# Layer 0's per-layer embedding moved from the end of the layer into its mixer, by way of memory

## The chip, the cores and the metric

The kernel runs on one core of a Trainium2 chip. Its engines work side by side, each through its own queue of instructions in order: TensorE (PE: matmuls and, listed as PEld, weight loads), VectorE (DVE), ScalarE (ACT), GpSimd (POOL) and SyncE (SP), which here issues nearly all the transfers (DMA). The metric is the device time of one execution in microseconds (us), lower is better. Times of several runs are given as their median.

## What is computed

One inference step of a two-layer encoder for 512 prompt rows and 32 sample rows (T = 544 columns in the kernel, which keeps features on partitions). Layer 0 has a mixer of a gated convolution and a state-space scan, then a convolutional feed-forward part; each layer ends with a gated embedding. Cut to what matters:

```python
z = hn @ W['w_even_in'][j]                       # 1024 -> 2048
gb, gc, xa, u = jnp.split(z, [A_WIDTH, 2 * A_WIDTH, 3 * A_WIDTH], axis=-1)
yc, new_hist = causal_dwconv(gc * xa, hist, W['w_conv_a'][j])
ya = gb * yc
yb, nr, ni = s5_mixer(u, ...)                    # scan over the rows, then a gate
y = jnp.concatenate([ya, yb], axis=-1) @ W['w_even_out'][j]
h = h + rmsnorm(y, W['g_mix_post'][i])
...
y = (jax.nn.gelu(gt) * val) @ W['w_ffn_down'][i]
h = h + rmsnorm(y, W['g_ffn_post'][i])
h = h + jax.nn.sigmoid(h @ W['w_ple_gate'][i]) * (pe[i] @ W['w_ple'][i])
```

The product `pe[i] @ W['w_ple'][i]` (256 features in, 1024 out) needs nothing that the layer computes.

## The kernel before

Every fp32 product is made of three matmuls on rounded operands: `mm_job` adds high x high (L131), low x high (L132) and high x low (L133) for each 128 rows of the sum. Weights come in units of 128x8x128: `prefetch` issues the load of `raw` on SP (L106), rounds it to `wh` on ACT (L107) and forms the rest `wl` on DVE (L108). The units are taken in the order of the list `units()`; four are kept at a time in the mixer, eight in the feed-forward part.

Columns are worked in two halves: half 0 is columns 0 to 255, half 1 columns 256 to 543 (288 wide). `phase(n, K, ...)` runs n weight units over both halves; half 1 of a unit is `delta` units behind half 0. A job is one unit on one half: 24 matmuls for K = 8. After each job it calls `run(rate)`, which advances the generators in the list `tasks` by that many steps, and takes results out of PSUM `lag` jobs late. So side work (norms, the scan) is spread over the jobs by counting calls; a scheduler then fixes each engine's order from when it thinks that operands are ready. An engine waits at the head of its queue, whatever stands behind.

Layer 0's mixer (`mixer_even`): phase(4) makes u. `shuffle` rearranges it on chip by 16 transfers on SP (`UUh`, L924). Then the generator `scan` runs beside phase(12), here called the a phase, whose 24 jobs make the convolution branch at rate 2. For each of eight pairs `scan` has `front` (matmuls `v`, L858; products `rt` with the rotation table E, L867 and L877; a scan instruction, L875; `sp`, L878 and L879) and `back` (matmuls `yp`, L891 and L893). It also makes its matrices: `prep_g` (transposes `tb`, L826, copied to `Bm` on ACT), `prep_c` (products Tm on DVE, copies `Cm` on ACT, L794) and `prep_t` (matmuls `tp`, L837, which need `Cm`). The table E is made by `rotations` on DVE, with copies on ACT. When all is done, the result of the scan is gated by matmuls on `GG`.

The tail of a layer (`tail`) ends with down products in three parts, then the embedding, then the gate. After the last part, `residual(half)` normalizes the down result y, adds it to h, and splits h into `Xh`, `Xl` for the gate, for eight slices k in turn (L338, L339, L323, L325). The embedding uses the unit p itself as the moving operand for half 0 (`pA`) and a copy with the sample rows attached for half 1 (`pB`), 8 jobs of 6 matmuls for each half, written to `e` by ACT (L472). The gate phase takes them in `c_gate` (L484).

Of the kernel before, what the change touches and what calls it, by code (L numbers as in the profile page):

```python
# [8 lines left out]
F32 = mybir.dt.float32  # L9
F32R = mybir.dt.float32r  # L10
I32 = mybir.dt.int32
AF = mybir.ActivationFunctionType
# [4 lines left out]
SEQ = 512  # L17
# [34 lines left out]

def units():

    u = [("w_even_in", i, 8) for i in range(16)]
    u += [("w_glu", i, 8) for i in range(2)]
    u += [("w_even_out", i, 8) for i in range(8)]
    for layer in range(2):
        for p, (a, b) in enumerate(FF_PARTS):
            u += [("w_up%d" % layer, i, 8) for i in range(2 * a, 2 * b)]  # L60
            u += [("w_down%d_%d" % (layer, p), i, b - a) for i in range(8)]
        u += [("p", layer, 8)]
        u += [("w_ple%d" % layer, i, 8) for i in range(2)]
        u += [("w_gate%d" % layer, i, 8) for i in range(8)]
        if layer == 0:
            u += [("w_odd_in", i, 8) for i in range(21)]
            u += [("w_odd_out", i, 8) for i in range(8)]
    return u
# [3 lines left out]
def trunk_kernel(ctx: ExitStack, tc: tile.TileContext, A: dict):  # L72
# [4 lines left out]
    main = ctx.enter_context(tc.tile_pool(name="main", bufs=1))  # L77
    small = ctx.enter_context(tc.tile_pool(name="small", bufs=2))
    mm = ctx.enter_context(tc.tile_pool(name="mm", bufs=3, space=PSUM))


    ulist = units()
# [5 lines left out]
    def wscope(n, extra=None):  # L88

        wsc.update(extra=extra, base=wsc["end"], end=wsc["end"] + n, ring=4 if extra is None else 8)  # L90
# [29 lines left out]
    def take(n):  # L120
        i = ucur[0]
        ucur[0] += n
        return list(range(i, i + n))
# [205 lines left out]
    def residual(half, h, y, st, gpost, gnext, rB=None):  # L329
# [18 lines left out]
            rB[half] = yield from s2.fin(D)  # L348
        waiting.discard(("r", half))


    def out_proj(layer, h, y, rB):

# [14 lines left out]
    def tail(layer, h, next_g):  # L368
# [2 lines left out]

        fs = ExitStack()
        ff = fs.enter_context(tc.tile_pool(name="ff%d" % layer, bufs=2))
        wscope(8 + 2 * NG + 24 + 11, fs.enter_context(tc.tile_pool(name="wf%d" % layer, bufs=4)))
        psc["extra"] = fs.enter_context(tc.tile_pool(name="fp%d" % layer, bufs=4, space=PSUM))
        psc["of"] = (7, 2)
        psc["st"] = fs.enter_context(tc.tile_pool(name="fs%d" % layer, bufs=1, space=PSUM))
# [11 lines left out]
        out_proj(layer, h, new_y(), rB)  # L389
        y = new_y()  # L390


        ps_r = ff.tile([128, 2, T - SEQ], F32, tag="psr", name="psr", bufs=1)
        nc.sync.dma_start(ps_r, A["ps"][layer])


        cg = [{}, {}]
# [54 lines left out]
        nc.sync.dma_start(A["o_ffn"][:, layer], fout[:, layer])  # L452


        us = take(3)
        prefetch(us[2])
        pA = [w_[:, :].rearrange("p (k t) c -> p k (t c)", k=2) for w_ in loaded[us[0]]]
        pB = [[ff.tile([128, T - 256], F32R, tag="ct%d" % i, name="pB", bufs=2) for k in range(2)] for i in range(2)]
        for k in range(2):
            for i in range(2):  # L460
                act.activation(pB[i][k][:, 0:256], pA[i][:, k, 256:512], AF.Copy)
            act.activation(pB[0][k][:, 256:], ps_r[:, k], AF.Copy)
            vec.tensor_tensor(pB[1][k][:, 256:], ps_r[:, k], pB[0][k][:, 256:], op=OP.subtract)
        emb = []
        for half, (c0, w) in enumerate(HALVES):
            e = ff.tile([128, 8, w], F32, tag="g%dh" % half, name="e", bufs=1)
            emb.append(e)
            xs = pA if half == 0 else pB
            for j in range(8):
                ps = ps_tile()  # L470
                mm_job(ps, us[1 + j // 4], range(2), xs[0], xs[1], 0, w, k0=2 * (j % 4))
                act.activation(e[:, j], ps[:, :w], AF.Copy, scale=0.5)  # L472
                run(j % 2)
        prefetch(us[2] + wsc["ring"])

        st = [Stat(0), Stat(1)]

# [40 lines left out]
    def mixer_even(h):  # L518
# [410 lines left out]
        task(scan())  # L929


        XCs = {}
        co = s5.tile([128, 4, 4], F32, tag="co", name="co")
        gct = [None, None]
# [420 lines left out]
        ms.close()  # L1355


    wscope(18)
    h = new_h()
    for half, (c0, w) in enumerate(HALVES):  # L1360
        for k0 in range(0, 8, 2 if half == 0 else 4):
# [157 lines left out]
```

## Time and profile before

| | us |
|---|---|
| runs, median of 3 (lowest to highest) | 1390.14 (1389.69 to 1393.61) |
| profiled execution | 1392.53 |
| its span (first to last instruction) | 1390.8 |
| PE busy | 1367.2 (98%) |
| DVE busy | 935.7 (67%) |
| ACT busy | 657.4 (47%) |

Busy is the time in which an engine executes, not its efficiency. In a timeline row the first number is the start from the span's start, the second the duration; `out<-in` are the kernel's names for the tiles, and a bracket at the end is idle time before the instruction with what ended it. Instructions of one engine overlap a little, so the step from start to start is shorter than a duration.

### The profile page before, as it was taken

The page shows a single profiled execution, that of the slowest core. Times are in us where ns is not written, and L with a number is a line of the kernel's source. Part 1 is how long each engine was busy: PE and PEld are TensorE (multiplying, and loading weights), DVE is VectorE, ACT ScalarE, POOL GpSimd, SP SyncE. Part 2 cuts the span into 40 slices and gives each one's busy share as a digit, 9 for nine tenths or more (in the row PEclk, how much of TensorE's full clock was granted, in tenths as well). Part 3 has the DMA queues.
Part 4 walks back from the last instruction along what each step waited for, and adds up shares of the span by engine and source line. Part 5 has one row for each costly group of instructions (what it writes and reads, how often), then busy time and mean ns, then how long its engine had stood idle before and what let it go on. Part 6 is the DMA issues. An engine that isn't in the chain of part 4 may idle for free.

```text
span 1390.8 us, 27437 instructions
## 1 busy us (share of the span) xinstructions
PE 1367.2 (98%) x10859; PEld 1344.2 (97%) x10859; DVE 935.7 (67%) x1968; ACT 657.4 (47%) x1314; POOL 198.3 (14%) x621
## 2 busy tenths in 40 slices
PE   8899999999999999999999999999999999999998
PEld 8798999999999999999998998999999999999998
DVE  9998738983477546868655555479843676368682
ACT  6653545543344223445547755465433343234451
POOL 1000000431022201300131100012320123013000
PEclk9999999999999999999999999999999999999999
DMA  6322352232312231331332332331223123313321
GB/s 199 94 67 63 117 184 77 77 96 72 122 62 86 97 122 39 105 113 53 99 94 70 117 109 64 108 107 62 92 92 122 46 92 107 99 50 94 100 73 50
DMA packets 49376, 128.26 MB, mean 92 GB/s; under 512 B 8368, under 2 KB 19896, under 8 KB 48992
## 3 DMA queue, kind: packets, MB, share of 16 engines
q1 hardware_dynamic: 47456, 124.35, 28.0%
q0 software_dynamic: 1792, 2.17, 0.7%
q8 instruction: 85, 1.39, 0.4%
q14 instruction: 43, 0.35, 0.1%
HBM read 116.93 MB, written 4.76 MB: 88 GB/s over the span
## 4 chain that ended last, share of the span: by engine, by line
PE 87%; DVE 8%; ACT 2%; SPq 1%; DMA 1%; issue 1%; POOL 0%; ACTq 0%; DVEq 0%
PE ps L131 27%; PE ps L133 27%; PE ps L132 27%; DVE wl L108 1%; SPq L924 1%; PE av L1254 1%; PE rp L307 1%; DVE Xl L327 1%; PE pp L1243 1%; DVE rg L875 1%; DVE rt L877 1%; ACT wh L107 1%; PE sc L1230 1%; DVE y L338 0%; DMA h<-in_x 0%
## 5 line engine op out<-in xcount | busy, mean ns | idle before, releaser
L131 PE MATMUL ps<-Xh,wh 128*128 128x256 f32 (+1 forms) x2512 | 728.1, 290 | 1.8 <-ACT wh L107 1.1
L133 PE MATMUL ps<-Xh,wl 128*128 128x256 f32 (+1 forms) x2512 | 725.5, 289 | 2.0 <-DVE wl L108 2.0
L132 PE MATMUL ps<-Xl,wh 128*128 128x256 f32 (+1 forms) x2512 | 725.6, 289 | 0.8 <-DVE Xl L327 0.5
L131 PEld LDWEIGHTS ps<-Xh,wh 128*128 128x128 f32 x2512 | 473.9, 189 | 4.4 <-ACT wh L107 1.6
L132 PEld LDWEIGHTS ps<-Xl,wh 128*128 128x128 f32 x2512 | 474.7, 189 | 3.0 <-DVE Xl L327 1.2
L133 PEld LDWEIGHTS ps<-Xh,wl 128*128 128x128 f32 x2512 | 473.0, 188 | 2.5 <-DVE wl L108 2.4
L108 DVE TENSOR_TENSOR wl<-raw,wh 128x1024 fp32r<-128x1024 f32 (+2 forms) x214 | 256.9, 1201 | 151.3 <-ACT wh L107 149.5
L107 ACT ACTIVATE wh<-raw 128x1024 fp32r<-128x1024 f32 (+2 forms) x214 | 222.1, 1039 | 248.3 <-PE ps L132 232.9
L131 PE MATMUL ps<-gh,wh 128*128 128x288 f32 (+1 forms) x704 | 203.5, 289 | 0.0
L133 PE MATMUL ps<-gh,wl 128*128 128x288 f32 (+1 forms) x704 | 203.4, 289 | 0.0
L132 PE MATMUL ps<-gl,wh 128*128 128x288 f32 (+1 forms) x704 | 202.5, 288 | 0.0
L132 PEld LDWEIGHTS ps<-gl,wh 128*128 128x128 f32 x704 | 133.5, 190 | 0.0
L131 PEld LDWEIGHTS ps<-gh,wh 128*128 128x128 f32 x704 | 133.0, 189 | 0.0
L133 PEld LDWEIGHTS ps<-gh,wl 128*128 128x128 f32 x704 | 132.9, 189 | 0.0
L278 ACT ACTIVATE t<-U,prm 128x256 f32<-128x256 f32 (+1 forms) x176 | 90.4, 517 | 71.0 <-DVE U L413 67.5
L279 DVE SCALAR_TENSOR_TENSOR t<-U,prm,t 128x256 f32<-128x256 f32 (+1 forms) x176 | 87.2, 498 | 34.9 <-ACT t L278 34.7
L413 DVE TENSOR_TENSOR U<-ps,rB 128x256 f32<-128x256 f32 (+1 forms) x176 | 76.6, 437 | 23.9 <-PE ps L133 19.8
L280 DVE SCALAR_TENSOR_TENSOR t<-U,prm,t 128x256 f32<-128x256 f32 (+1 forms) x176 | 87.5, 501 | 4.5
L416 POOL COPY hca<-U 128x2 f32<-128x2 f32 x88 | 24.3, 277 | 366.2 <-DVE U L413 366.1
L423 ACT ACTIVATE t<-t 128x288 f32<-128x288 f32 (+1 forms) x88 | 37.7, 429 | 81.6 <-DVE t L280 81.5
L439 DVE TENSOR_TENSOR y<-y,ps 128x256 f32<-128x256 f32 (+1 forms) x64 | 27.9, 436 | 62.0 <-PE ps L133 62.0
L429 ACT ACTIVATE gh<-t 128x288 fp32r<-128x288 f32 (+1 forms) x88 | 37.4, 425 | 67.3 <-DVE t L427 67.3
(272 smaller groups left out, 1376.7 us busy)
## 6 DMA issues: line engine op xcount, KB each, us to landing
raw<-in_w_up SPq DMA_DIRECT2D x88, 512.0 KB, 3.4
raw<-in_w_down SPq DMA_DIRECT2D x32, 512.0 KB, 3.4
raw<-in_w_odd_in SPq DMA_DIRECT2D x21, 512.0 KB, 3.6
raw<-in_w_gate SPq DMA_DIRECT2D x16, 512.0 KB, 4.0
raw<-in_w_even_in SPq DMA_DIRECT2D x15, 512.0 KB, 3.7
raw<-in_w_down SPq DMA_DIRECT2D x16, 384.0 KB, 3.1
raw<-in_w_even_out SPq DMA_DIRECT2D x8, 512.0 KB, 4.0
raw<-in_w_odd_out SPq DMA_DIRECT2D x8, 512.0 KB, 3.5
```

The source lines that it names most:

```text
L107: act.activation(wh[:, k], raw[:, k], AF.Copy)
L108: vec.tensor_tensor(wl[:, k], raw[:, k], wh[:, k], op=OP.subtract)
L131: pe.matmul(ps[:, :n], wh[:, k0 + k, :], h_, start=(i == 0), stop=False)
L132: pe.matmul(ps[:, :n], wh[:, k0 + k, :], l_, start=False, stop=False)
L133: pe.matmul(ps[:, :n], wl[:, k0 + k, :], h_, start=False, stop=(i == last))
L278: act.activation(t, v[2], AF.Copy, scale=w(2))
L279: vec.scalar_tensor_tensor(t, v[1], w(1), t, op0=OP.mult, op1=OP.add)
L280: vec.scalar_tensor_tensor(t, v[0], w(0), t, op0=OP.mult, op1=OP.add)
L413: vec.tensor_tensor(block_view(U, half)[2], like(ps, half), like(rB[half], half), op=OP.mult)
L423: act.activation(t, t, AF.Gelu_apprx_tanh)
L429: act.activation(gh[:, f - f0], g, AF.Copy)
L439: vec.tensor_tensor(yk, yk, ps, op=OP.add)
```

## The change

Layer 0's embedding is computed in the mixer, between phase(4) and the a phase, by a new function `embed`; layer 1's stays where it is and uses the same function. In the mixer the first eight jobs cover columns 0 to 287 (all from p), the other eight 288 to 543 (from `pB`, a buffer of the pool that the scan uses too). After each of the 16 jobs ACT writes `e` (one of three buffers), SP stores it to `emb0` in memory, and `run(1)` advances the scan by a step. In the tail two loads bring `emb0` back as `emb`. The units p and w_ple0 move to behind the fourth w_even_in unit.

```diff
-    u = [("w_even_in", i, 8) for i in range(16)]
+    u = [("w_even_in", i, 8) for i in range(4)]
+    u += [("p", 0, 8)]
+    u += [("w_ple0", i, 8) for i in range(2)]
+    u += [("w_even_in", i, 8) for i in range(4, 16)]
...
+    emb0 = dram.tile([128, 8, T], F32, tag="emb0", name="emb0")
...
+    def embed(ps_, pB, n0, put):
+
+        us = take(3)
+        prefetch(us[2])
+        pA = [w_[:, :].rearrange("p (k t) c -> p k (t c)", k=2) for w_ in loaded[us[0]]]
+        m = SEQ - n0
+        for k in range(2):
+            for i in range(2):
+                act.activation(pB[i][k][:, 0:m], pA[i][:, k, n0:SEQ], AF.Copy)
+            act.activation(pB[0][k][:, m:T - n0], ps_[:, k], AF.Copy)
+            vec.tensor_tensor(pB[1][k][:, m:T - n0], ps_[:, k], pB[0][k][:, m:T - n0], op=OP.subtract)
+        for n, (c0, w) in enumerate(((0, n0), (n0, T - n0))):
+            xs = pB if n else pA
+            for j in range(8):
+                ps = ps_tile()
+                mm_job(ps, us[1 + j // 4], range(2), xs[0], xs[1], 0, w, k0=2 * (j % 4))
+                put(n, j, c0, w, ps[:, :w])
+        prefetch(us[2] + wsc["ring"])
...
+        emb = [ff.tile([128, 8, w], F32, tag="g%dh" % half, name="e", bufs=1) for half, (_, w) in enumerate(HALVES)]
+        if layer == 0:
+            for half, (c0, w) in enumerate(HALVES):
+                nc.sync.dma_start(emb[half], emb0[:, :, c0:c0 + w])
+        else:
...
+            embed(ps_r, pB, 256, put_e)
...
+        ps_r = s5.tile([128, 2, T - SEQ], F32, tag="psr", name="psr")
+        nc.sync.dma_start(ps_r, A["ps"][0])
+        pB = pt([128, 2, 2, 256], "pB").bitcast(F32R)
+
+        def put_e(n, j, c0, w, ps):
+            e = small.tile([128, T - 256], F32, tag="sq", name="e", bufs=3)[:, :w]
+            act.activation(e, ps, AF.Copy, scale=0.5)
+            nc.sync.dma_start(emb0[:, j, c0:c0 + w], e)
+            run(1)
+
+        embed(ps_r, [[pB[:, i, k] for k in range(2)] for i in range(2)], 288, put_e)
```

Three places of the engines' orders. First SP's queue at the sixteen `UUh` moves that bring u into the scan's layout, before:

```order
L966 DMA hcs<-in_cache_ffn 128x176
L106 DMA raw<-in_w_even_in 128x1024 x5
L924 DMA UUh<-UUh 32x4x137 x16
L106 DMA raw<-in_w_even_in 128x1024 x2
L845 DMA Tm<-Tm 32x4x96
```

and of the change:

```order
L998 DMA hcs<-in_cache_ffn 128x176
L112 DMA raw<-in_w_ple 128x1024 x2
L112 DMA raw<-in_w_even_in 128x1024 x2
L958 DMA emb_69<-e 128x288 x3
L112 DMA raw<-in_w_even_in 128x1024
L943 DMA UUh<-UUh 32x4x137 x16
L958 DMA emb_69<-e 128x288 x5
L958 DMA emb_69<-e 128x256 x6
L112 DMA raw<-in_w_even_in 128x1024 x2
L864 DMA Tm<-Tm 32x4x96
```

Three stores and the weight load that was the last of five stand ahead of the moves now, the other stores behind them.

Second, PE at the end of the scan: the last `yp` among the a phase's matmuls (ps<-X), before:

```order
L891 MATMUL yp<-sp,Cm 128x137
L893 MATMUL yp<-UUh,Tm 128x137
L891 MATMUL yp<-sp,Cm 128x137 x2
L893 MATMUL yp<-UUh,Tm 128x137
L132 MATMUL ps<-Xl,wh 128x288
```

and of the change:

```order
L137 MATMUL ps<-Xh,wh 128x256
L910 MATMUL yp<-sp,Cm 128x137 x2
L912 MATMUL yp<-UUh,Tm 128x137
L910 MATMUL yp<-sp,Cm 128x137 x2
L912 MATMUL yp<-UUh,Tm 128x137
L138 MATMUL ps<-Xl,wh 128x256
```

From the last of these rows to the first matmul on `GG` stand 152 matmuls of the a phase before (104 of 288 columns, 48 of 256), and 335 in the change (192 and 143).

Third, PE between the last down matmul (ps<-gh) and the gate of layer 0, where L314 and L320 belong to the residual of half 0 and the rp<-ones,sq of the change to the statistics of half 1; before:

```order
L133 MATMUL ps<-gh,wl 128x288
L314 MATMUL rp<-cst,rc 128x128 x2
L131 MATMUL ps<-wh 128x256
L132 MATMUL ps<-wl,wh 128x256
L133 MATMUL ps<-wh,wl 128x256
```

and of the change:

```order
L139 MATMUL ps<-gh,wl 128x288
L320 MATMUL rp<-cst,rc 128x128 x2
L313 MATMUL rp<-ones,sq 128x1 x3
L137 MATMUL ps<-Xh,wh 128x256 x6
L138 MATMUL ps<-Xl,wh 128x256
```

The 96 matmuls of the embedding, of which ps<-wh is the first, are gone from there; the gate's matmuls on `Xh` follow at once.

## Rows read from the trace of the kernel before

**Rows 1.** The page's first lines: span; busy time of each engine (share) xinstructions

```profile
span 1390.8 us, 27437 instructions
PE 1367.2 (98%) x10859; PEld 1344.2 (97%) x10859; DVE 935.7 (67%) x1968; ACT 657.4 (47%) x1314; POOL 198.3 (14%) x621
```

**Rows 2.** Windows: length, busy (xinstructions) of PE, PEld, DVE, ACT, POOL; clock, DMA, GB/s

```profile
38.50:136.50 98.00, 87.27 (x683) 83.70 (x681) 90.57 (x183) 51.13 (x107) 1.03 (x10) 0.97 0.26 73
136.50:156.00 19.50, 19.50 (x154) 19.50 (x153) 13.22 (x25) 9.85 (x22) 0.00 (x0) 1.00 0.35 104
624.10:636.40 12.30, 12.30 (x100) 12.30 (x99) 11.58 (x28) 10.99 (x28) 0.00 (x0) 1.00 0.29 88
```

**Rows 3.** PE's waits, 38.5 to 136.5 us: us in total, times, longest

```profile
PE tp L837 <- ACT Cm L794: 4.5, 1, 4.5
```

**Rows 4.** Timeline of DVE: start us, us, engine, line, operation, shapes

```profile
42.61 0.22 DVE L593 TENSOR_TENSOR UUh<-ps,rB 128x32 f32<-128x32 f32 x1
57.35 1.29 DVE L867 TENSOR_TENSOR rt<-v,E 128x1096 f32<-128x1096 f32 x1
...
134.68 0.44 DVE L879 TENSOR_TENSOR sp<-rt 128x274 f32<-128x274 f32 x1
```

**Rows 5.** Window of the scan on DVE: length, busy (xinstructions), clock, DMA, GB/s

```profile
57.35:134.87 77.52, 70.19 (x131) 0.96 0.21 62
```

**Rows 6.** Timeline of PE: first matmuls of both embedding parts and of the gate

```profile
624.25 0.36 PE L131 MATMUL ps<-wh 128*128 128x256 f32 x1
...
630.08 0.30 PE L131 MATMUL ps<-pB,wh 128*128 128x288 f32 x1
...
636.48 0.28 PE L131 MATMUL ps<-Xh,wh 128*128 128x256 f32 x1
```

**Rows 7.** Timeline of DVE at the end of layer 0's down phase

```profile
626.42 0.48 DVE L338 SCALAR_TENSOR_TENSOR y<-y,prm,rB 128x256 f32<-128x256 f32 x1
...
634.65 1.23 DVE L108 TENSOR_TENSOR wl<-raw,wh 128x1024 fp32r<-128x1024 f32 x1
635.79 0.76 DVE L325 TENSOR_TENSOR Xl<-h,Xh 128x256 fp32r<-128x256 f32 x2
```

**Rows 8.** Timeline of SP's queue, and the chain that ended last, near 42 us

```profile
42.47 0.33 SPq L106 DMA_DIRECT2D raw<-in_w_even_in  x1
42.91 11.27 SPq L924 DMA_DIRECT2D UUh<-UUh  x16
...
52.09 1.92 DMA UUh<-UUh
```

**Rows 9.** Instructions on tile e; and the page's DMA issues

```profile
L472 ACT ACTIVATE e<-ps x16: 367/390/447, 625.7 to 637.5; 128x256 f32<-128x256 f32 x8, 128x288 f32<-128x288 f32 x8
...
raw<-in_w_gate SPq DMA_DIRECT2D x16, 512.0 KB, 4.0
```

**Rows 10.** Timeline of PE at 47 us and of ACT at 55 us

```profile
47.02 1.09 PE L826 MATMUL tb<-cst,G 128*128 128x128 f32 x8 [1.29 <-ACT G L821]
...
54.90 0.71 ACT L755 ACTIVATE E<-E 128x252 f32<-128x252 f32 x2
```

**Rows 11.** Groups of DVE in the scan: busy us, mean ns | idle before

```profile
L941 DVE TENSOR_TENSOR gct<-ps,rB 128x288 f32<-128x288 f32 (+1 forms) x6 | 2.5, 423 | 0.0
```

**Rows 12.** Timeline of PE behind the last yp; instructions on tile GG

```profile
136.65 0.29 PE L133 MATMUL ps<-Xh,wl 128*128 128x288 f32 x1
...
L131 PE MATMUL ps<-GG,wh x32: 284/290/294, 156.1 to 167.9; 128*128 128x274 f32 x32
```

**Rows 13.** Windows with the granted clock; timeline of PE at tp

```profile
60.00:65.00 5.00, 1.70 (x14) 1.50 (x12) 5.00 (x8) 2.45 (x4) 0.00 (x0) 0.89 0.00 0
65.00:70.00 5.00, 3.81 (x17) 2.87 (x18) 5.00 (x11) 3.59 (x6) 0.11 (x1) 0.50 0.00 0
70.00:75.00 5.00, 5.00 (x39) 5.00 (x40) 5.00 (x12) 2.35 (x4) 0.00 (x0) 0.93 0.42 128
...
66.19 3.62 PE L837 MATMUL tp<-Cm,g 128*32 128x128 f32 x16 [4.48 <-ACT Cm L794]
```

More of the change, by code (lines that the diff above doesn't have):

```diff
@@ L61, in units @@
             u += [("w_down%d_%d" % (layer, p), i, b - a) for i in range(8)]
-        u += [("p", layer, 8)]
-        u += [("w_ple%d" % layer, i, 8) for i in range(2)]
+        if layer == 1:
+            u += [("p", 1, 8)]
+            u += [("w_ple1", i, 8) for i in range(2)]
         u += [("w_gate%d" % layer, i, 8) for i in range(8)]
@@ L79, in trunk_kernel @@
     mm = ctx.enter_context(tc.tile_pool(name="mm", bufs=3, space=PSUM))
+    dram = ctx.enter_context(tc.tile_pool(name="dram", bufs=1, space=bass.MemoryType.DRAM))
+    emb0 = dram.tile([128, 8, T], F32, tag="emb0", name="emb0")
     ulist = units()
@@ L373, in tail @@
         ff = fs.enter_context(tc.tile_pool(name="ff%d" % layer, bufs=2))
-        wscope(8 + 2 * NG + 24 + 11, fs.enter_context(tc.tile_pool(name="wf%d" % layer, bufs=4)))
+        wscope(8 + 2 * NG + 24 + (11 if layer else 8), fs.enter_context(tc.tile_pool(name="wf%d" % layer, bufs=4)))
         psc["extra"] = fs.enter_context(tc.tile_pool(name="fp%d" % layer, bufs=4, space=PSUM))
@@ L390, in tail @@
         y = new_y()
-        ps_r = ff.tile([128, 2, T - SEQ], F32, tag="psr", name="psr", bufs=1)
-        nc.sync.dma_start(ps_r, A["ps"][layer])
+        if layer:
+            ps_r = ff.tile([128, 2, T - SEQ], F32, tag="psr", name="psr", bufs=1)
+            nc.sync.dma_start(ps_r, A["ps"][layer])
         cg = [{}, {}]
@@ L452, in tail @@
         nc.sync.dma_start(A["o_ffn"][:, layer], fout[:, layer])
[L455 to L472, printed above, removed]
+        emb = [ff.tile([128, 8, w], F32, tag="g%dh" % half, name="e", bufs=1) for half, (_, w) in enumerate(HALVES)]
[3 more added lines that the diff above has]
+        else:
+            pB = [[ff.tile([128, T - 256], F32R, tag="ct%d" % i, name="pB", bufs=2) for k in range(2)]
+                  for i in range(2)]
+            def put_e(n, j, c0, w, ps):
+                act.activation(emb[n][:, j], ps, AF.Copy, scale=0.5)
                 run(j % 2)
-        prefetch(us[2] + wsc["ring"])
+            embed(ps_r, pB, 256, put_e)
         st = [Stat(0), Stat(1)]
@@ L929, in mixer_even, with put_e @@
         task(scan())
+        ps_r = s5.tile([128, 2, T - SEQ], F32, tag="psr", name="psr")
+        nc.sync.dma_start(ps_r, A["ps"][0])
+        pB = pt([128, 2, 2, 256], "pB").bitcast(F32R)
+        def put_e(n, j, c0, w, ps):
+            e = small.tile([128, T - 256], F32, tag="sq", name="e", bufs=3)[:, :w]
[3 more added lines that the diff above has]
+        embed(ps_r, [[pB[:, i, k] for k in range(2)] for i in range(2)], 288, put_e)
         XCs = {}
@@ L1355, in mixer_odd @@
         ms.close()
-    wscope(18)
+    wscope(21)
     h = new_h()
```

## The prediction

> **What bounds the kernel now.** I read the page first: TensorE (PE) is busy 1367.2 of 1390.8 us [rows 1], so whatever takes PE's time off its path is worth that time, and an engine beside it costs nothing until PE waits for it. Next I read the busy time by stage, to see whether PE is as full where the work goes as where it leaves. It isn't. From the end of the u projection to the end of the scan (38.5 to 136.5 us) PE is busy 87.27 of 98.0 us and VectorE (DVE) 90.57; in the rest of the a phase (136.5 to 156) PE is busy all of its 19.5 us, and so it is in the embedding at 624.1 to 636.4 [rows 2]. The largest wait of PE in the scan stage is 4.5 us, before `tp` [rows 3]. The reader is to see that two works run side by side here: a scan, whose chain is DVE's, and the a phase, which fills PE while the scan's few matmuls wait in the same queue. The last u result is written at 42.61, the first product of the scan (`rt`, L867) starts at 57.35, and the last `sp` (L879) ends at 135.1 [rows 4]. Between those two DVE is busy 70.19 of 77.52 us [rows 5]: it, not PE, says when the scan ends. I call that end T.
>
> **The matmuls that move.** 48 matmuls of 256 columns start at 624.25, 48 of 288 at 630.08, and the first of the gate at 636.48 [rows 6]: 5.83 and 6.40 us, so 0.121 and 0.133 us each, 12.2 us in all. The mixer gets 48 of each width again, so PE's total work stays. What counts is what lies under which wait, before and after.
>
> **Tail of layer 0: 12.2 us leave, about 9 come back.** Before, the embedding ran on PE while DVE did `residual(0)`: its first instruction starts at 626.42, its last pair at 635.79, which ends at 636.55, with one weight split (`wl`, 634.65 to 635.79 by starts) among them [rows 7]. The gate's first job needs that result, slice k for its k-th triple. By the order of the change nothing but the statistics of half 1 stands between the last down matmul and the gate, and no `wl` stands inside the residual. So it ends 1.1 us earlier, near 635.4, the last triple follows, and the job ends near 635.8. Before, it began at 636.48 and took 24 x 0.121 = 2.9 us, to 639.4. The tail gives 639.4 - 635.8 = 3.6 us; half 1's statistics may take a little of it, so I count **-3.1**. Bounds: nothing, and the whole -12.2, if the residual could start so much earlier; its start hangs on the statistics of the last down results, and nothing in the change moves those.
>
> **The scan's start: about +3.** In SP's order of the change three stores of `e` and one weight load now stand ahead of the sixteen `UUh` moves. The third store needs the third `e`, and on ScalarE (ACT) that stands behind the E copies of rotation step 3, another `e` and a G copy. Before, the moves began at 42.91, right behind the last u result, took 11.27 us on SP, and the last landed at 52.09 + 1.92 = 54.0 [rows 8]. Now the last u result comes some 0.5 us later (one more pair of rotation products is ahead of it), E copies, G and two `e` take about 1.9 us on ACT and DVE (an `e` 0.39 [rows 9]), a store and a load about 1 us of SP (11.27 / 16 = 0.7, and 0.33 for a load [rows 8]): moves from 46.4, landed near 57.5. From there PE needs the first `v` matmul and the second `tb` group (1.09), ACT the `Bm` and E copies (1.0 and 0.7) [rows 10], because in the new order `tb` stands behind that `v`, and E behind `Bm`. `rt` can start near 60.4 instead of 57.35: +3.0. Bounds: 0, if DVE has as much other work as before until then, and +6, if `e` waits for its three buffers too (the nearest transfers land in 2 to 4 us).
>
> **The scan itself: about -3.5.** By DVE's order, between the first `rt` and the last `sp` stand 18 instructions of the a phase instead of 30, and two more E products. 12 x 0.37 us from start to start (the group has a mean of 0.42 with overlap [rows 11]) is -4.4, the two E products +0.9. DVE's waits in the stretch, 77.52 - 70.19 = 7.3 us [rows 5], I leave as they are; bounds: they vanish (-7.3) or double (+7.3). T then moves by 3.0 - 3.5 = **-0.5 us**.
>
> **What is left to do at T: +23.2.** This is the term that decides. The scan takes a step at each call of `run`: two per a job (24 matmuls, 3.0 us of PE), but one per embedding job (6 matmuls, 0.76 us). So sixteen of its steps now come with 16 x 0.76 = 12.2 us of PE work beside them, where before they had 16 x 1.5 = 24. PE's order shows it: before, 152 matmuls of the a phase stand behind the last `yp` (104 of 288, 48 of 256); now 335 do (192 and 143). The 152 took from 136.65 to the first GG matmul at 156.1, 19.45 us [rows 12]; the steps of 0.133 and 0.121 give 19.6 for them and 42.8 for the 335: **+23.2**, of which 12.2 is the embedding's time and 11.0 is work that no longer lies beside the scan. PE's idle time in the scan stage should double, from 10.7 to some 21 us.
>
> **The clock: +1.** After the 4.48 us wait before `tp` the granted clock stands at 0.50 from 65 to 70 and is 0.89 and 0.93 in the fives beside it [rows 13]: (0.11 + 0.50 + 0.07) x 5 = 3.4 us of full-speed time lost, most of it while PE waits or does `tp` (3.62 us for 16 matmuls). The longer waits can add such stretches, one in the mixer and one in the tail; the waits themselves are long gone on DVE's path, so I take 1, with 0 and 2 x 3.4 as bounds. The Trainium skill (TensorE: Matmul & The Clock Gate, section "HAM oscillation — how this bites in real kernels") says that waits between bursts of matmuls put the array back to its half rate each time, so that a wait costs more than itself. The trace agrees at 65 to 70; priced fully at both places that rule would make the sum 5.8 us larger.
>
> **Costed at nothing.** The two loads of `emb0` (1.0 and 1.2 MB): at the pace of a gate weight, 512 KB in 4.0 us [rows 9], 8 and 9 us. The first can start once half 0 of the down phase is done, seven jobs (7 x 18 x 0.133 = 17 us) before that phase ends, the second at 624, and half 1 of the gate needs it near 652 (5.7 jobs of 2.9 us after 635.8). Without that cover each us late is a us. The three weight units of the embedding take the a phase's ring slots, but sooner than the a phase asks for its fourth unit.
>
> **Sum.** -3.1 - 0.5 + 23.2 + 1 = **+20.6 us**. The profiled execution took 1392.53 us, 1.7 over its span and 2.4 over the median of the runs, 1390.14; the sum is a difference, so on the median it gives **1410.7 us**, +1.5%.
>
> **Rivals.**
> 1. *The gaps are filled; not slower.* PE's 10.7 us of idle in the scan stage [rows 2] swallow the embedding: mixer +12.2 - 10.7 = +1.5, tail -3.1: 1388.5 us, no change to measure; if the residual were also free in the tail, 1379.4. For it speaks that PE waits only where the work goes. Against it: T would have to come some 20 us earlier, at 114.5, while DVE alone has 66.7 us of work from the first `rt` on: 57.35 + 66.7 = 124. It decides at that point, T before 114.5. Chance 0.08 (0.04 same, 0.04 faster). The Trainium skill (Perfetto Trace Analysis, section "Optimization Strategy") advises to interleave stretches in which different engines are the most contended, which is this rival; the trace says that the place was already interleaved, with the a phase.
> 2. *The scan gains, or the tail does.* With fewer a results DVE's 7.3 us of waits vanish, or the tail keeps most of its 12.2: 1403 or 1401 us. For it: some of those waits are for PE. Chance 0.22.
> 3. *A new wait in the mixer.* Three `e` buffers, the store behind sixteen moves on the same queue, and ACT stuck at an `e` with the scan's copies behind it: T +7 and the clock +6, 1424 us. Chance 0.12.
> The forecast has 0.58.
>
> **Range.** A measurement here can tell about 0.3%, 4 us. The forecast's own bounds of a few us a term give some 1404 to 1417; to leave out no more than 2 in 10 it must take in rival 2 and half of 3: 1400 to 1421. Faster 0.04, same 0.04, slower 0.92.
>
> **What would show it.** Right: in the new profile some 14 a jobs run on a full PE after the last `yp`; GG starts 20 to 25 us later than 156.1; the `UUh` moves end near 57 or later; PE idles some 8 to 10 us between the last down matmul and the end of the gate's first job. Wrong: T far ahead of 130, a tail that closes without a gap, or a wait before GG for weights held up by the second set of moves on SP.

## The result, and the profile after

| | before | after |
|---|---|---|
| runs, median of 6 each (lowest to highest), us | 1392.34 (1389.69 to 1393.96) | 1400.62 (1399.32 to 1402.67) |
| span of the profiled execution, us | 1390.8 | 1399.1 |
| start of the first GG matmul | 156.05 | 171.15 |
| last instruction of PE's down phase of layer 0 | 624.12 | 637.73 |
| first matmul on `nid`, in layer 1's mixer | 718.0 | 726.5 |

The change makes the kernel slower: ratio 1.0064, 95% interval [1.0054, 1.0074], 8 to 9 us. The sign was forecast, the size was not: +20.6 was predicted. The table says where the time went: +15.1 up to GG, -1.5 from there to the end of the down phase, -5.1 in the tail, and -0.2 behind it, +8.3 in all.

The page's first lines after:

```profile
span 1399.1 us, 27490 instructions
PE 1370.5 (98%) x10859; PEld 1346.7 (96%) x10859; DVE 936.1 (67%) x1968; ACT 656.4 (47%) x1314; POOL 197.4 (14%) x621
```

PE has the same 10859 matmuls as in [rows 1], and is idle 28.6 us instead of 23.6. Where, two windows show (length; busy time and instructions of PE, PEld, DVE, ACT, POOL; clock; DMA share; GB/s). Before:

```profile
36.00:64.00 28.00, 24.41 (x197) 23.91 (x195) 28.00 (x73) 19.78 (x39) 0.11 (x1) 1.00 0.42 116
64.00:136.00 72.00, 64.86 (x500) 61.79 (x501) 64.67 (x123) 33.86 (x73) 0.93 (x9) 0.95 0.21 60
```

After:

```profile
36.00:64.00 28.00, 18.25 (x123) 16.58 (x122) 27.89 (x74) 22.95 (x47) 0.10 (x1) 0.87 0.49 144
64.00:136.00 72.00, 69.56 (x549) 66.84 (x549) 60.99 (x112) 37.01 (x82) 0.86 (x9) 0.98 0.27 79
```

The idle time has moved forward. At the scan's start, where the embedding now stands, PE idles 9.8 us instead of 3.6; behind 64 it idles 2.4 instead of 7.1. DVE has next to no gap at the start in either. So PE's idle time from 36 us to GG is 12.2 us, against 10.7; with the 12.2 us of embedding and some 1.2 more lost at the half clock (the busy time of each 4 us times what its clock lacks: 3.5 against 2.3) that makes the +15.1 but for 0.2.

The scan in the timeline of DVE after:

```profile
42.73 0.21 DVE L612 TENSOR_TENSOR UUh<-ps,rB 128x32 f32<-128x32 f32 x1
...
54.44 1.30 DVE L886 TENSOR_TENSOR rt<-v,E 128x1096 f32<-128x1096 f32 x1
...
126.88 0.42 DVE L898 TENSOR_TENSOR sp<-rt 128x274 f32<-128x274 f32 x1
```

Against [rows 4] the last u result stands where it stood, the first `rt` starts 2.9 us earlier, and T, the end of the last `sp`, is 127.3 instead of 135.1. SP's queue shows why the first of these is not the delay that was forecast:

```profile
40.83 1.78 SPq L958 DMA_DIRECT2D emb<-e  x3
42.72 0.39 SPq L112 DMA_DIRECT2D raw<-in_w_even_in  x1
43.20 10.43 SPq L943 DMA_DIRECT2D UUh<-UUh  x16
```

The three stores are ahead of the moves, but they are done by the time that u is: the moves start 0.3 us later than in [rows 8]. Behind T, the timeline of PE and the instructions on GG:

```profile
128.54 0.37 PE L138 MATMUL ps<-Xl,wh 128*128 128x256 f32 x1
...
L137 PE MATMUL ps<-GG,wh x32: 284/290/294, 171.1 to 183.0; 128*128 128x274 f32 x32
```

From that row to GG it is 42.6 us against the 19.45 of [rows 12]: +23.1, as counted. The longest waits of PE between 36 us and GG (engine, line, waited for; us, times, longest):

```profile
PE ps L137 <- ACT e L957: 4.0, 1, 4.0
PE tb L845 <- ACT G L840: 3.3, 3, 1.2
PE v L877 <- DVE rt L886: 2.7, 1, 2.7
PE yp L910 <- ACT GG L1009: 0.9, 1, 0.9
```

The wait at `tp` [rows 3] is gone and a wait for an `e` stands in its place. The timeline of ACT ahead of that `e`:

```profile
56.23 1.58 ACT L774 ACTIVATE E<-E 128x756 f32<-128x756 f32 x2 [1.89 <-DVE E L770]
57.72 1.06 ACT L891 ACTIVATE sp<-seg,sb 128x274 f32<-128x274 f32 x2
59.29 1.27 ACT L813 ACTIVATE Cm<-Tm 64x512 f32<-64x512 f32 x2 [0.51 <-DVE Tm L810]
60.58 0.99 ACT L957 ACTIVATE e<-ps 128x288 f32<-128x288 f32 x3
```

ACT waits for DVE's products E and Tm, and the copies that would free PSUM for the next embedding jobs stand behind them in its order (e4 below shows that the stores have a part in that order). In the tail, the timeline of PE, and two windows of it:

```profile
637.73 0.38 PE L320 MATMUL rp<-cst,rc 128*128 128x128 f32 x2
640.93 1.44 PE L313 MATMUL rp<-ones,sq 128*128 128x1 f32 x6 [2.82 <-DVE sq L304]
642.23 0.99 PE L137 MATMUL ps<-Xh,wh 128*128 128x256 f32 x3
```

```profile
640.00:645.00 5.00, 4.07 (x19) 4.07 (x20) 5.00 (x15) 1.59 (x4) 0.00 (x0) 0.56 0.74 245
645.00:650.00 5.00, 5.00 (x35) 5.00 (x35) 4.26 (x13) 1.59 (x4) 1.07 (x1) 0.76 0.03 11
```

PE waits only 3.6 us there (0.8 of it for `rc`), then takes the slices of several gate jobs in turn as the residual makes them; the clock costs 0.44 x 4.07 + 0.24 x 5 = 3.0 us of its busy time. 12.2 - 3.6 - 3.0 = 5.6, near the gain of 5.1.

### The profile page after: what moved, and what is told of

Read it like the earlier page. It is cut to its first block, busy times and chain, and to the rows that moved or that the text cites. A ratio compares the mean times of both kernels' runs of the same rounds, so it can differ in the third digit from the quotient of the medians.

```text
span 1399.1 us, 27490 instructions
## 1 busy us (share of the span) xinstructions
PE 1370.5 (98%) x10859; PEld 1346.7 (96%) x10859; DVE 936.1 (67%) x1968; ACT 656.4 (47%) x1314; POOL 197.4 (14%) x621
## 4 chain that ended last, share of the span: by engine, by line
PE 88%; DVE 8%; ACT 2%; issue 1%; POOL 1%; DMA 0%; SPq 0%; ACTq 0%; DVEq 0%; POOLq 0%
PE ps L137 27%; PE ps L138 27%; PE ps L139 27%; DVE wl L114 2%; PE av L1286 1%; DVE Xl L333 1%; ACT wh L113 1%; PE rp L313 1%; PE pp L1275 1%; PE sc L1262 1%; PE yp L910 1%; PE tp L856 0%; DVE y L344 0%; DVE h L345 0%; PE sc L1347 0%
## 5 line engine op out<-in xcount | busy, mean ns | idle before, releaser
L137 PEld LDWEIGHTS ps<-gh,wh 128*128 128x128 f32 x704 | 132.9, 189 | 0.0
L139 PEld LDWEIGHTS ps<-gh,wl 128*128 128x128 f32 x704 | 132.9, 189 | 0.0
```

Of the source, the lines that this page charges most:

```text
L137: pe.matmul(ps[:, :n], wh[:, k0 + k, :], h_, start=(i == 0), stop=False)
L139: pe.matmul(ps[:, :n], wl[:, k0 + k, :], h_, start=False, stop=(i == last))
```

## The experiments

Times are medians of 4 to 11 runs (before: 6 to 15), with the ratio to before on the same chip; u, T and GG are the end of the last u result, of the last `sp`, and the start of the first GG matmul in the profiled execution.

| kernel | median us | ratio [95%] | u | T | GG |
|---|---|---|---|---|---|
| before | | | 42.8 | 135.1 | 156.1 |
| after | 1400.62 | 1.0064 [1.0054, 1.0074] | 42.9 | 127.3 | 171.1 |
| e1_tail_alone | 1384.03 | 0.9950 [0.9936, 0.9965] | 42.6 | 133.7 | 154.7 |
| e2_mixer_alone | 1408.84 | 1.0119 [1.0105, 1.0133] | 44.6 | 128.1 | 171.9 |
| e3_no_steps | 1400.65 | 1.0066 [1.0053, 1.0079] | 44.6 | 152.3 | 173.3 |
| e4_no_store | 1399.70 | 1.0056 [1.0044, 1.0068] | 45.2 | 127.3 | 170.2 |
| e5_wl_pool_after | 1420.95 | 1.0204 [1.0190, 1.0218] | 48.0 | 143.4 | 190.3 |
| e6_wl_pool_before | 1402.24 | 1.0067 [1.0055, 1.0080] | 48.6 | 143.8 | 167.3 |
| e7_split | 1399.18 | 1.0047 [1.0033, 1.0061] | 44.3 | 133.3 | 165.9 |
| e8_split_pool | 1414.01 | 1.0153 [1.0139, 1.0167] | 49.3 | 148.7 | 183.8 |
| e9_late | 1404.10 | 1.0088 [1.0075, 1.0101] | 44.3 | 135.8 | 174.8 |
| e10_run2 | 1403.26 | 1.0080 [1.0066, 1.0095] | 45.1 | 126.4 | 174.6 |
| e11_sp_twice | 1400.19 | 1.0067 [1.0054, 1.0080] | 44.8 | 132.9 | 173.4 |
| e12_e_on_dve | 1407.67 | 1.0117 [1.0101, 1.0134] | 45.2 | 136.3 | 180.3 |
| e13_late_buffers | 1399.14 | 1.0056 [1.0044, 1.0068] | 44.1 | 135.7 | 168.6 |
| e14_no_wl_after | 1403.10 | 1.0086 [1.0071, 1.0100] | 40.7 | 128.3 | 173.8 |
| e15_no_wl_before | 1384.55 | 0.9950 [0.9938, 0.9962] | 41.3 | 127.8 | 149.7 |
| e16_add_pool_before | 1394.74 | 1.0023 [1.0013, 1.0033] | 44.5 | 139.3 | 160.3 |
| e17_no_wl_no_steps | 1399.54 | 1.0059 [1.0045, 1.0072] | 42.1 | 147.8 | 169.7 |
| e18_split_late | 1392.51 | 1.0008 [0.9999, 1.0017] | 44.2 | 135.3 | 162.0 |

How near two profiled executions can be read: from u to GG it is 113.2 us before and 112.1 in e1, which has the same mixer, and 128.2 in the change and 127.3 in e2. So differences of about 1 us between two traces say nothing. Nor does the late u of most rows. In e2, e3, e4, e7, e9 to e13, e16 and e18 it comes 1.3 to 2.3 us later than before or in the change, in e17 1.4 later than in e14. Each of these traces has a dip of the granted clock before 36 us that costs 1.4 to 1.7 us (shown in the last section); before, the change, e1, e14 and e15 have none there. Where it matters, GG is therefore counted from u below.

**The two halves of the change: e1, e2.**

```diff
-        embed(ps_r, [[pB[:, i, k] for k in range(2)] for i in range(2)], 288, put_e)
...
-                nc.sync.dma_start(emb[half], emb0[:, :, c0:c0 + w])
+                nc.sync.dma_start(emb[half], A["x"][:, :, c0:c0 + w])
```

> Leaves out layer 0's embedding altogether: the two loads in the tail bring back the layer's input x in its place, everything else in the mixer is as before. So it is the tail of the change alone. The prediction's step says -3.1 us (12.2 us leave, 9 come back because the gate's first job waits for the residual). The trace of the change shows -5.3 us between the end of layer 0's down products and the odd mixer (+13.6 before, +8.3 behind), because the gate's jobs run slice by slice beside the residual; by that this kernel takes 5.3 us less than before, about 1387. Rival: nothing in the tail waits, -12.2, about 1380, which would mean that the mixer of the change costs over 20.

The other half keeps the mixer's call and gives the tail its own embedding back:

```diff
-        if layer:
+        if True:
...
-        if layer == 0:
+        if False:
             for half, (c0, w) in enumerate(HALVES):
                 nc.sync.dma_start(emb[half], emb0[:, :, c0:c0 + w])
```

> The embedding is computed and stored in the mixer as in the change, and a second time in the tail as before, which uses its own result (the stored one is not read). So it is the mixer of the change alone. If the two parts add, it costs what the change's trace shows at the start of GG, +15.0, less about 1.7 of the clock's dip near 230 us that is gone there: +13 to +15, 1405 to 1407. The record's terms for the mixer (-0.5 + 23.2 + 1) would be +23.7, about 1416.

The tail alone gains 0.5%, some 7 us; in its trace the stretch from the end of the down phase to `nid` is 6.3 shorter, with the same 2.8 us wait of PE as in the change. The mixer alone costs 1.2%, 16.5 us: above the 13 to 15 read from the trace, and far from the record's 23.7. The parts add: +1.19% - 0.50% = +0.69%, against +0.64% for the change.

**What sets GG, first: the scan's steps: e3, e10, e11.**

```diff
             nc.sync.dma_start(emb0[:, j, c0:c0 + w], e)
-            run(1)
```

> The change without the call run(1) after each of the embedding's jobs in the mixer: the sixteen steps of the scan then come with the a phase's jobs, two for 3 us of matmuls, as before. Theory of pacing (the steps taken beside 0.76-us jobs leave 11 us of a phase work for the end): about 152 matmuls of the a phase again behind the last yp, T about 8 us later than in the change, GG some 9 us earlier than 171.1, 1390 to 1394 us in all. Rival (T follows from VectorE's work alone, so calls don't matter; the embedding simply adds its 12.2 us and the waits stay): GG at 168 to 171, 1398 to 1401.

The rival held, and more sharply than it said. The timeline of DVE and the instructions on GG in the kernel without steps:

```profile
58.12 1.29 DVE L886 TENSOR_TENSOR rt<-v,E 128x1096 f32<-128x1096 f32 x1
...
151.82 0.44 DVE L898 TENSOR_TENSOR sp<-rt 128x274 f32<-128x274 f32 x1
...
L137 PE MATMUL ps<-GG,wh x32: 284/290/294, 173.3 to 185.1; 128*128 128x274 f32 x32
```

T is 25 us later, the matmuls left behind it take 19.5 us instead of 42.6, just as the calls have it, and the time is the same; from u to GG it is 128.7 us against 128.2. T and what is left behind it are two ends of one stretch of PE's work; neither is a price.

```diff
-            run(1)
+            run(2)
```

> The change with run(2) for run(1) after each embedding job in the mixer, so that the scan's steps come still earlier; by the order, the matmuls behind the last yp then stand for about 48 us instead of 43.5. By the record's sum (T from VectorE's work, and behind it what is left) GG comes 4 us later than in the change, 1404 to 1406. By the theory formed after the kernel without steps (GG follows from all of TensorE's work and the waits at the scan's start, whatever is left at T) T comes some 4 us earlier and GG within 2 us of 171.1: 1399 to 1402.

T comes 0.9 us earlier and GG 3.4 later, but u is 2.2 later already: from u, T is 3.1 earlier and GG 1.2 later. The median lies between the two, 1403.3. Inconclusive by itself.

```diff
             vec.tensor_tensor(sp[:, 0, :, 1:M + 1], t4[:, 0, 0], t4[:, 1, 1], op=OP.subtract)
             vec.tensor_tensor(sp[:, 1, :, 1:M + 1], t4[:, 0, 1], t4[:, 1, 0], op=OP.add)
+            vec.tensor_tensor(sp[:, 0, :, 1:M + 1], t4[:, 0, 0], t4[:, 1, 1], op=OP.subtract)
+            vec.tensor_tensor(sp[:, 1, :, 1:M + 1], t4[:, 0, 1], t4[:, 1, 0], op=OP.add)
```

> The change with the two instructions that write sp done twice for each of the eight pairs, with the same result: 16 more instructions of 0.44 us on VectorE, 7.0 us, all on the scan's chain. By the order, 40 us of matmuls stand behind the last yp instead of 43.5. If VectorE says when the scan ends and what is left follows, T moves by +7 and GG by +3.5: 1404. If TensorE has other work while it waits for the scan, T moves by some 3.5 to 7 and GG by less than 1.5: 1400 to 1402.

T moves by 5.6 us, 3.7 of them counted from u, and the time does not: 1400.2. From u to GG it is 128.6 us, in the change 128.2. This work on DVE behind the scan's start has cover.

**What sets GG, second: work on DVE at the scan's start: e12, e14, e15, e17, and GpSimd in e5, e6, e8, e16.**

```diff
-            act.activation(e, ps, AF.Copy, scale=0.5)
+            vec.tensor_scalar(e, ps, 0.5, None, op0=OP.mult)
```

> The change with the sixteen copies of e in the mixer on VectorE instead of ScalarE. In the change's trace TensorE waits once 4.0 us for an e on ScalarE, between 50 and 60. Theory 1 (ScalarE's queue, where e stands among the scan's copies, is what the embedding costs beyond its work): the wait goes, GG 2 to 4 us earlier, 1397 to 1399. Theory 2 (VectorE's preparation of the scan, without a gap from 36 to 75, is what TensorE waits for in one form or another): 16 copies of about 0.37 us stand in that preparation, GG 3 to 6 us later, 1403 to 1407.

Theory 2, by 7 us. PE's waits up to GG:

```profile
PE ps L137 <- DVE e L957: 6.0, 3, 4.5
PE tb L845 <- ACT G L840: 4.4, 4, 2.2
```

The wait for `e` followed the copies to DVE and grew: whichever engine empties PSUM for the embedding is busy with the scan's matrices there.

```diff
-            wl = wp.tile([128, 8, 128], F32R, tag="wl", name="wl", bufs=4)
+            wl = wh if 4 <= len(loaded) < 19 else wp.tile([128, 8, 128], F32R, tag="wl", name="wl", bufs=4)
...
-                vec.tensor_tensor(wl[:, k], raw[:, k], wh[:, k], op=OP.subtract)
+                if wl is not wh:
+                    vec.tensor_tensor(wl[:, k], raw[:, k], wh[:, k], op=OP.subtract)
```

The kernel before has 12 such units instead of 15, so there the bound is 16.

> The change without the subtractions that form wl of the 15 units from the fifth to the end of the a phase: the third matmul uses wh in place of wl, so TensorE's work stays and the result is not the reference's. VectorE loses four instructions of 1.22 us between 36 and 75 and some before and behind. If VectorE's preparation is what TensorE waits for there, the time from the last u result to GG falls by 3 to 5 us, 1396 to 1398 in all. If TensorE's order alone counts: within 1 us of the change, 1400.

> The kernel before without the subtractions that form wl of its 12 units from the fifth to the end of the a phase (wh takes wl's place in the third matmul; the result is not the reference's). It too loses four of 1.22 us between 36 and 75. If VectorE's preparation bounds the stretch before as well, 3 to 5 us less than before, 1387 to 1389, and the change's extra is not in these instructions. Rival: within 1 us of before.

The kernel before gains 0.5% [0.4, 0.6], some 7 us, and its window at the scan's start has no idle time of PE left:

```profile
36.00:64.00 28.00, 28.00 (x229) 27.64 (x228) 28.00 (x72) 23.57 (x45) 0.21 (x2) 1.00 0.36 104
```

The longest wait of before, 4.5 us at `tp` [rows 3], is gone. So DVE's work did bound this stretch before. The change with the same edit is not faster but slower (1.0086 against 1.0064): u comes 2.2 us earlier and GG 2.6 later, so from u to GG it takes 133.1 instead of 128.2, with 4.5 us of waiting at `v` for `rt`, 3.6 at `tb` and 3.2 for `e`. Both theories put to that run failed.

> The change without the calls run(1) in the mixer's embedding and without the subtractions for wl of 15 units (wh takes wl's place in the third matmul; the result is not the reference's). If the early calls are why less work on VectorE didn't help the change, it helps here: from the last u result to GG 123 to 125.5 us instead of the 128.5 of the kernel without steps alone, 1394 to 1396. If the scan's start is slow for another reason, 128 or more, 1399 to 1403.

It takes both edits (e14's and e3's). From u to GG 127.6 us and 1399.5, nearer the second theory: the early calls are not the reason either.

```diff
-                vec.tensor_tensor(wl[:, k], raw[:, k], wh[:, k], op=OP.subtract)
+                weng = pool_e if 4 <= len(loaded) < 19 else vec
+                weng.tensor_tensor(wl[:, k], raw[:, k], wh[:, k], op=OP.subtract)
```

> The change with the subtraction that makes wl done on GpSimd instead of VectorE for the 15 weight units from the fifth to the end of the a phase (p and w_ple0 among them). From 36 to 75 us of the change VectorE is busy without a gap and makes four of them at 1.22 us, while TensorE is busy 24.3 of 39 us. Theory (it is VectorE's preparation of the scan that holds the scan's first matmuls, and TensorE's queue behind them): TensorE's idle time there shrinks by about 5 us, GG near 166, 1395 to 1397. Rival (VectorE isn't what TensorE waits for, or GpSimd takes so long for a unit that the a phase waits for its weights): 1400 or more.

> The kernel before with the same edit for its 12 units from the fifth to the end of the a phase. Before, TensorE idles 10.7 us between 38.5 and 136.5, 4.5 of it ahead of tp, while VectorE has no gap from 36 to 80. By the theory that VectorE's preparation of the scan is the cause the time falls by 3 to 5 us, 1386 to 1389; by the rival it stays at 1391 or rises.

Both got much slower, and u itself came 5 to 6 us later: GpSimd took 2.4 us for a unit (DVE 1.22), and at times held DVE up while it did (last section). These two, and e8, don't answer the question.

```diff
-                    vec.tensor_tensor(src, src, t[:, 1], op=OP.add)
+                    pool_e.tensor_tensor(src, src, t[:, 1], op=OP.add)
```

> The kernel before with the four additions that make Tm from its two products (128x512, 0.69 us each on VectorE) on GpSimd, which is idle there; nothing is left out. If VectorE's preparation is what tp waits for, TensorE's 4.5 us wait shrinks by up to 2.7 us: 1389 to 1391 against 1392. Rival: GpSimd takes twice as long (2.4 us against 1.2 for a wl) and Cm waits for it, so tp comes 1 to 3 us later: 1392 to 1394.

The rival, and a little more: +0.23%; GpSimd's median for an addition was 2.5 us, and `tp` waits 4.5 us as before.

**The stores, and other places: e4, e7, e8, e9, e13, e18.**

```diff
-            nc.sync.dma_start(emb0[:, j, c0:c0 + w], e)
...
-                nc.sync.dma_start(emb[half], emb0[:, :, c0:c0 + w])
+                nc.sync.dma_start(emb[half], A["x"][:, :, c0:c0 + w])
```

> Leaves out the sixteen stores of the embedding to memory; the loads in the tail read the layer's input x in its place. All the products and copies stay. If the round trip through memory is hidden, as the record has it, the time is that of the change, 1400.6, within 1 us. Rival: the stores hold up the moves of UUh on SP's queue and the three buffers of e hold up ScalarE (one wait of 4.0 us of PE for an e in the change's trace): 1395 to 1398 without them.

Within 1 us of the change, so the round trip through memory costs next to nothing in time. But it does shape the start. The two windows without stores:

```profile
36.00:64.00 28.00, 25.29 (x193) 23.93 (x193) 26.78 (x76) 26.79 (x62) 0.11 (x1) 1.00 0.37 98
64.00:136.00 72.00, 65.64 (x503) 61.95 (x503) 65.08 (x118) 34.78 (x75) 0.87 (x9) 0.98 0.25 72
```

PE idles 2.7 us at the scan's start instead of 9.8, and 6.4 behind it instead of 2.4. ACT's order is another: copies of `e` now stand ahead of the long copy of E.

```profile
58.04 1.20 ACT L957 ACTIVATE e<-ps 128x256 f32<-128x256 f32 x4
59.83 1.57 ACT L774 ACTIVATE E<-E 128x756 f32<-128x756 f32 x2
```

The wait for `e` shrinks to 1.4, but PE then waits 3.2 us for `wl` on DVE, behind 70 us. From u to GG it is 125.0 us instead of 128.2, which the time does not show, as u comes 2.2 later.

```diff
-        embed(ps_r, [[pB[:, i, k] for k in range(2)] for i in range(2)], 288, put_e)
+        embed(None, None, 256, put_e, (0,))
```

> Only the first eight jobs of the embedding (columns 0 to 255, 5.8 us) are done in the mixer and stored; the other eight (288 columns, 6.4 us) stay in the tail, where the residual needs some 4 us of cover. p and w_ple0 are loaded and rounded twice. If the moved matmuls cost the mixer their own time and the share of the extra waits, and the tail gains their whole time (it keeps cover enough), the two nearly cancel: 5.8 + 1.5 - 5.8, 1391 to 1394. Rival 1: the waits of the mixer take the eight jobs in, 1386 to 1388. Rival 2: the extra waits and the half clock come with the first embedding job already: 1395 to 1397.

Rival 2, and a little more: 1399.2. From u to GG it is 121.7 us, 8.5 more than before, for eight jobs of 5.8 us; the change has 15.0 more for 12.2. So the extra of some 3 us is there with the first eight jobs already. The rest of its loss over before lies at the kernel's start (u 1.5 us later, with the clock's dip there) and in the spread of its runs: the profiled execution, 1394.7 us long, was a quick one.

> The split version with wl on GpSimd for the units from the fifth to the end of the a phase. If VectorE's preparation is what makes TensorE wait in the mixer, the gain of that edit adds to the split version's time (3 to 5 us less than that); if it isn't, the two are equal within 1 us.

Slower, as the other two with `wl` on GpSimd.

```diff
         finish()
         nc.sync.dma_start(A["o_ssm"], so)
+        embed(ps_r, [[pB[:, i, k] for k in range(2)] for i in range(2)], 288, put_e)
```

> The change with the whole embedding computed at the end of the mixer, behind the a phase and the scan and ahead of GG, where TensorE has no waits to fill; its units p and w_ple0 follow the a phase's. Then the mixer should cost its 12.2 us and nothing else, with the waits of before beside the scan, and the tail gives back what it gave alone (8.4 us by the medians): 1392 + 12.2 - 8.4 = 1395.8, 1394 to 1398. That would show that the place beside the scan costs some 4 us more than the work. Rival: beside the scan a part of the embedding does lie in waits, and late it costs more than in the change: 1402 or more.

1404.1: the rival's number, but not its reason. With the next edit:

```diff
-            e = small.tile([128, T - 256], F32, tag="sq", name="e", bufs=3)[:, :w]
+            e = Cm.rearrange("p a q t c -> p (a q t c)")[:, 288 * (8 * n + j):288 * (8 * n + j) + w]
```

> The kernel with the embedding late (behind the a phase and the scan), but each of the sixteen e has a place of its own in the space of Cm, which is free by then, instead of one of three buffers. In the late kernel TensorE waited 4.3 us for e and ran part of the stretch at half clock. If the three buffers (each freed by its store's landing) were the cause, the embedding now costs its 12.2 us: from the last u result to GG some 125.5 us instead of 130.5, and 1392 + 12.2 - 8.4 = 1396, 1394 to 1398 in all. Rival (it is the place: ScalarE, or the first use of p): still 1402 to 1405.

The window from the last `yp` to GG, with three buffers and then with sixteen places:

```profile
137.40:174.80 37.40, 33.38 (x247) 32.94 (x247) 19.20 (x33) 19.32 (x44) 0.00 (x0) 0.95 0.46 140
```

```profile
137.40:168.50 31.10, 31.10 (x247) 31.10 (x246) 19.29 (x33) 19.71 (x45) 0.00 (x0) 1.00 0.53 157
```

The same 247 matmuls, 4 us of waiting and the half clock behind it gone: 6.3 us. GG is 12.5 us later than before, and 11.2 counted from u: about the embedding's bare 12.2, where the change pays 15.0. In all 1399.1, +0.56%, above the expected 1394 to 1398, with a span of 1396.1: the profiled execution was a quick one. By its time e13 can't be told from the change (+0.64%).

> The first eight jobs of the embedding at the end of the mixer with a place for each e (12.4 us for all sixteen there by e13, so some 5.9 for these), the other eight (6.4 us) in the tail. The residual leaves TensorE some 4 us idle when no embedding is there, so 6.4 us of it are cover enough and the tail gains 5.8: no change against before, 1391 to 1393. Rival: the tail gains only in proportion (8.4 x 5.8 / 12.2 = 4.0): 1393 to 1395.

The first theory: 1392.5, no change against before that can be told. The tail without half of its embedding has no idle PE at all and no dip of the clock, as before:

```profile
600.00:660.00 60.00, 60.00 (x481) 59.88 (x481) 46.95 (x105) 30.79 (x67) 1.54 (x2) 1.00 0.32 106
```

No version beat the kernel before without leaving work out.

## Why the prediction was right in sign and wrong in size

- **What is left to do at T, +23.2: measured +23.1, and yet no price.** The count was right, its use was not. The record took T as set by DVE and the rest as following it, so a larger rest was a loss. e3 has the old rest and the new time; e11 moves T and not the time. What costs, beside the embedding's own 12.2 us, is PE's idle time and its half clock up to GG. The record's "PE's idle time in the scan stage should double, from 10.7 to some 21 us" is where this shows: it went to 12.2, which in PE's terms is 9 of the 12.3 us between forecast and result. In the terms of the record's sum the same miss is T's, in the next two items: -0.5 was forecast, -7.8 came.
- **The scan's start, +3: measured -2.9. This is the step of the sum that failed, by 5.9 us.** It let `rt` wait for the last of the sixteen `UUh` moves, and the moves for the third `e`. Neither held. The third `e` did not wait behind the E copies of rotation step 3, the stores were issued at 40.83, and `UUh` moved at once. And the first `rt` needs only a part of the moves: the `v` ahead of it start at 49.62 and 52.18, while moves are issued until 53.6. Even before, `v` started at 53.63, ahead of the landing at 54.0 that the record counted from. What fills the stretch from u to `rt` is DVE, without a gap but for 0.1 us. Rows of before and then of the change:

```profile
55.28 1.22 DVE L108 TENSOR_TENSOR wl<-raw,wh 128x1024 fp32r<-128x1024 f32 x1
56.41 0.55 DVE L751 TENSOR_TENSOR E<-ya 128x384 f32<-128x384 f32 x1
```

```profile
49.62 0.50 PE L877 MATMUL v<-UUh,Bm 128*128 128x137 f32 x2 [0.25 <-ACT Bm L847]
55.65 0.55 DVE L770 TENSOR_TENSOR E<-ya 128x384 f32<-128x384 f32 x1
```

By DVE's rows, before had there a weight split (1.1 us from start to start), a pair of E products (0.9) that now stands behind `rt`, two results of the a phase (0.7), and a pair of rotation products (0.7) that now stands ahead of u; new are 0.2 for `pB`. That is the 3.0 us: 14.5 from the end of u to `rt` in before, e9 and e13, 11.5 in the change, e2, e10 and e11.
- **The scan itself, -3.5: measured -4.9.** From `rt` to T DVE is busy 66.6 of 72.9 us instead of 70.2 of 77.5 [rows 5]: 3.6 less work, near the 3.5 counted, and 1.0 less waiting.
- **The tail, -3.1: measured -5.1, mis-sized.** The record let one gate job wait for the whole residual. The scheduler gave PE slices of several gate jobs instead, so PE idled 3.6 us, not 8 to 10. The half clock took 3.0 more, near the 3.4 that the record had for one dip.
- **The clock, +1.** Mixer and tail paid more of it (1.2 and 3.0, which are in the terms above), but a dip that before had near 230 us is gone; that is the -1.5 between GG and the end of the down phase.
- **Costed at nothing:** the loads of `emb0` held nobody up: the trace has no wait for them.

With the measured sizes the sum closes: -2.9 - 4.9 + 23.1 - 5.1 - 1.5 = +8.7, against +8.3 in the spans; 0.3 of the difference lies between T and the last `yp`.

The sign was right because the embedding's 12.2 us found no cover in the mixer and the tail gave back less than that; the term that was to decide it is no price. Of the record's signs of being right only the first came, some 14 a jobs behind the last `yp` (42.6 us): GG came 15.1 later and not 20 to 25, the moves ended at 53.6 and not near 57, PE idled 3.6 us in the tail and not 8 to 10. Of its signs of being wrong one came: T, at 127.3, is ahead of 130.

**The rivals.** Rival 1 (gaps filled) is out: PE's idle time did not fall, and from u to GG the change pays 15.0 us for 12.2, more than e13's 11.2 at a place where next to nothing can be filled. Rival 2 came nearest, with T at -7.8, just its number, but that is luck: it had DVE's 7.3 us of waits vanish, and they went to 6.3; the earlier start did the most. Rival 3's wait exists (4.0 us for `e`), without its price. In the trace ACT stood behind copies that wait for DVE, and not behind a store. Yet without the stores that order is gone (e4), so the three buffers, whose stores stand behind the sixteen moves, do have a part in it. That the scheduler put `e` late because of them is argued, not shown.

**What stays open.** That DVE's preparation bounds the scan's start of the kernel before is shown (e15). For the change it isn't: less work on DVE didn't help (e14, e17), nor did leaving out the stores (e4), nor fewer calls (e3). Each left or uncovered another wait of PE, at `e`, `v` or `tb` in the same place or at `wl` behind it. Why an embedding there waits more than the a phase did is argued from the rows, not shown: an embedding job fills a place in PSUM in 0.76 us, an a job in 3.0, so the same few places hide a quarter of the delay of ACT or DVE. Two of the waits taken away together, stores and `wl`, was not tried, nor was a place of its own for each `e` at the scan's start, which e13 had at the end of the mixer.

## What to carry over

When work is moved beside a stretch where one engine is the bound, sum up the idle time and the clock of the engine that carries the whole kernel, from the last common point to the next; a count of what is left behind a chain's end is no price, since a later end leaves less. Work made of short jobs can be a poor filler for a place where the engines that empty PSUM are late: here it filled none of the 10.7 us and paid some 3 more than its bare time, with the first half of its jobs already. Few buffers for its results, each free only when its store has landed, can cost as much as the place: 6.3 us between e9 and e13. And work that covers a wait in the tail need not be all of it: half was enough, so the other half is worth its full time elsewhere, if there is a place that takes it for less.

## What the runs showed of the hardware

GpSimd held VectorE up. In the kernel before with `wl` on GpSimd, a DVE instruction on 16 elements a lane (0.18 us in the kernel before) took 2.41 us and ended with the GpSimd instruction beside it. Its timelines of DVE and of GpSimd:

```profile
49.82 2.41 DVE L743 TENSOR_SCALAR ya<-ya 128x16 f32<-128x16 f32 x1
...
49.01 3.14 POOL L109 TENSOR_TENSOR wl<-raw,wh 128x1024 fp32r<-128x1024 f32 x1 [3.68 <-DMA raw<-in_w_even_in]
```

Both end near 52.2. The Trainium skill (SBUF — State Buffer, section "Who interferes with whom") says that the two share one pair of ports, which one instruction holds to its end while the other stands; this row agrees. It is not so for each pair: a product for Tm at 49.21, beside the first part of the same GpSimd instruction, took its usual 0.69 us.

The same wait can cost a dip of TensorE's clock or none. Both kernels idle some 0.5 us between 225 and 230 (PE busy 4.52 and 4.48 of 5). The window behind it, before and then in e1:

```profile
230.00:235.00 5.00, 5.00 (x30) 4.79 (x29) 3.58 (x10) 2.22 (x5) 1.85 (x7) 0.66 0.00 0
```

```profile
230.00:235.00 5.00, 5.00 (x44) 5.00 (x44) 4.88 (x14) 2.76 (x8) 1.63 (x5) 1.00 0.00 0
```

The granted clock is 0.66 in the one and full in the other, 30 matmuls against 44: 1.7 us that no edit of the change explains. The Trainium skill (TensorE: Matmul & The Clock Gate, section "HAM oscillation — how this bites in real kernels"), which the prediction leaned on, describes waits between bursts of matmuls that put the array back to its half rate (1.2 GHz) each time. Its example has longer waits than these; here a short one did so once and once not.

The same is what moves u. A window in which PE waits for a weight unit, 0.72 and 1.06 us in the change, then 0.67 and 1.12 in e13, in work that neither edit is about:

```profile
10.00:15.00 5.00, 3.21 (x24) 2.81 (x24) 4.98 (x12) 3.53 (x6) 0.00 (x0) 1.00 1.04 351
```

```profile
10.00:15.00 5.00, 3.21 (x18) 2.80 (x18) 4.98 (x12) 3.10 (x5) 0.00 (x0) 0.81 0.93 285
```

The dip of e13 goes on behind 15 us, at 0.85 to 20, and costs 1.7 us in all. The spread of the runs goes with such dips: of the 14 runs of before beside e13, the quickest, 1389.5 us, has a mean granted clock of 0.998, the slowest, 1394.4 us, of 0.995.
